# Retention values of heads 0 and 1 by seven block products ahead of the core, kept split in DRAM, with the core's heads overlapping by two chunks

## The chip, the cores and the metric

The kernel runs on one core of a Trainium2 chip. The metric is the device time of one execution in microseconds (us). TensorE is written PE, VectorE DVE, ScalarE ACT, GpSimd POOL and SyncE SP.

## The reference

A trunk of two layers works on 1024 tokens of width 1024, in fp32. Each layer has a mixer (layer 0 a gated delta net, layer 1 a retention) and a gated FFN with a short convolution, each followed by a residual and a layer norm; inputs of mixer and FFN are scaled and shifted by vectors computed from a condition `c`. The change lies in the retention of layer 1, 4 heads with 256 features in q and k and 512 in v, cut into 8 chunks of 128 tokens:

```
q, k, v, gate = jnp.split(h @ w_in, [H * dk, 2 * H * dk, 2 * H * dk + H * dv], axis=-1)
...
scores = jnp.einsum('bhncd,bhnmd->bhncm', q, k) * dmask[None, :, None]
intra = jnp.einsum('bhncm,bhnmv->bhncv', scores, v)
...
    o = jnp.einsum('bhck,bhkv->bhcv', q_n, state) * xi[None, :, :, None]
    state = (state * gamma_c[None, :, None, None]
             + jnp.einsum('bhck,bhcv->bhkv', k_n * zeta[None, :, :, None], v_n))
...
o = _standardize(o, 1e-6).reshape(b_, s, H * dv)
o = o * jax.nn.silu(gate.astype(F32))
return o.astype(h.dtype) @ w_out
```

The state passes from chunk to chunk, so the chunks of one head follow each other; heads are independent.

## The kernel before, in words

**Split operands.** An fp32 product is made of three fast matmuls: each operand is split into a high part (ACT copies it into the rounded type, L89) and a low part (DVE subtracts, L90), and low x high, high x low and high x high are summed in PSUM (`split` L88, `mm3` L108, `mma` L312).

**Seven products.** The projections for the gate and for q and k run as a 2 x 2 block product with seven instead of eight products (`strassen`, L1334). It leaves the blocks `B` of the normalized input in SBUF: 11 and 21 are the first half of the tokens (`hTb` buffers, also called `h0`), 22 the second half's upper features, T1 to T4 sums and differences (`hTa`, `aux`, `qkv`). q and k go through the rotation to DRAM (`qd`), the gate through silu to DRAM (`gd`). Then `hT[1]`, the second half of the tokens, is completed by transposing four loaded tiles `xlo`.

**The core's program.** The retention core is written as generators, which a small planner (`run`, L758) interleaves: it keeps a clock of the matmuls issued so far (`pm` and `pq` add their assumed cost), each generator yields a delay or an event that it waits for, and of those that are due the one with the lowest number goes next. The order that results on PE is fixed by dependencies (`pq`, L736). `core(h)` makes the recurrence of head h, `ret_back` the normalization and output of one chunk, and `ret_fill` is the filler that takes PE whenever no core step is due: the values of a head (`ret_v`), and behind them the first two of seven products of the out-projection (`proj_gen`). A fixed number of `qkv` buffers, counted by `take` and `give`, limits how far values run ahead: 20 buffers, two per chunk of values.

**Values.** `ret_v(h, half)` multiplies half of the tokens with the head's weights: 8 contraction tiles x 4 token tiles x 3 = 96 matmuls of 512 columns, into four `acc` banks. Four splits then give the values `vv` of four chunks, high and low. Heads 0 to 3 and two halves make 768 matmuls.

**One chunk of the core.** Two halves of the state update (3 matmuls each, `sc<-vv,kz`, each into a bank of the tag `sc`, of which there are two), read by DVE into `Sr`; the scores and transposed keys of the next chunk (`mm<-qk`, `mm<-cst,qk`) with `kz`, `sT`, `sThl`; the transposes of the chunk before (`mm<-cst,on`); the output (`sc<-vv,sThl` x3 and `sc<-Sr,qk` x2, the latter in full fp32) into an `sc` bank. `ret_back`: bn_stats and its aggregate on DVE, the power -1/2 on POOL (L2026), `on` on DVE (L2030), which frees the bank; four transposes, product with the gate (`ot`, L2051), stores to DRAM (`od`); for chunks 4 to 7 POOL forms four sums of blocks (L2062) for the out-projection, the fourth after the first store has landed.

Before, `core(h)` waits for the first values of its head and for the end of `core(h - 1)`.

Of the kernel before, what the change touches and what calls it, by code (L numbers as in the profile page):

```python
# [9 lines left out]
F32 = mybir.dt.float32  # L10
F32R = mybir.dt.float32r
# [4 lines left out]
P = 128  # L16
D = 1024
# [16 lines left out]
def trunk_kernel(ctx: ExitStack, tc, A):  # L34
# [11 lines left out]
    def tl(tag, shape, dt=F32, name=None):  # L46
        return sb.tile(shape, dt, tag=tag, name=name or tag, bufs=BUFS[tag])
# [34 lines left out]
    def hs(half):  # L82
        return slice(half * HALF, (half + 1) * HALF)
# [4 lines left out]
    def split(dst_h, dst_l, src, eng=dve):  # L88
        anchor["sp"] = act.activation(dst_h, src, AF.Copy)  # L89
        eng.tensor_tensor(dst_l, src, dst_h, ALU.subtract)  # L90
# [211 lines left out]
    def build_hT(tag, xts, scale, shift, fr=range(KT)):  # L302
        return [build_one(tag, xts, scale, shift, f) for f in fr]
# [503 lines left out]
    def give(tag, n):  # L807
        free[tag] += n
# [1106 lines left out]
    gates_ = [gate_item(u) for u in range(4, 16, 2)]  # L1915
    mixed = [(ropes if q == "r" else gates_).pop(0) for q in "rrgrgrrgrgrrgg"]
    B = strassen(h0, xts, sc_r, sh_r, [gate_item(0), gate_item(2)] + mixed, ("hTa", "aux", "qkv", "qkv", "hTa"), True)
    hT = [h0, []]
    xlo = []
    for t in range(4):  # L1920
# [2 lines left out]
        with after(("out", 0)):  # L1923
            sp.dma_start(x, xs[1][r0:r0 + P, 0:HALF])
        xlo.append(x)
    hT[1] = build_hT("hTa", xlo, sc_r, sh_r, range(4)) + B["22"]

    def ret_v(h, half):
        accs = acc4()
        for kp in range(4):  # L1930
            wh, wl = load_w(A["ret_wv"][h, kp])
            if (h, half, kp) == (RH - 1, 1, 3):
                yield after_ev(("qk", h))
                start_out()
# [38 lines left out]
        return r  # L1973

    def core(h):
        yield after_ev(("rv", h, 0), ("core", h - 1))
        if h == 1:
            bg_ada(1, 2, "row")
        q, k = load_qk(h, 0), load_qk(h, 1)
        emit(("qk", h))  # L1980
        St = None
        yield RL["q"]
        r = ret_front(h, 0, q, k)
        yield RL["f"]
        for n in range(NCH):
            if n == 4:
                yield after_ev(("rv", h, 1))
            vh, vl = va[h][n]
            Sn = None
            if n < NCH - 1:  # L1990
                kz = r["kz"]
                Sn = tl("lane", [P, 2, HALF], name="Sr")
                for j in range(2):
                    js = slice(j * P, (j + 1) * P)
                    p2 = sc_tile()
                    pm(p2, kz[:, 1, js], vh, start=True, stop=False)
                    pm(p2, kz[:, 0, js], vl, start=False, stop=False)
                    pm(p2, kz[:, 0, js], vh, start=False, stop=True)
                    if n == 0:
                        dve.tensor_copy(Sn[:, j], p2)  # L2000
                    else:
                        dve.scalar_tensor_tensor(Sn[:, j], St[:, j], gamma_c[h], p2, ALU.mult, ALU.add)
# [11 lines left out]
            give("qkv", 2)  # L2014
            yield [(-0.1, ret_back(h, n, po))]
            yield RL["c"]
            St, r = Sn, rn
        emit(("core", h))

    def ret_back(h, n, po):  # L2020
        st = tl("st", [P, 2, 6], name="rst")
        dve.bn_stats(st[:, 0], po)
        mv = tl("s8", [P, 4], name="mv")
        dve.bn_aggr(mv[:, 0:2], st[:, 0])
        dve.tensor_scalar(mv[:, 2:3], mv[:, 1:2], 1e-6, None, ALU.add)
        pool.tensor_tensor(mv[:, 3:4], mv[:, 2:3], mhalf[:, 0:1], ALU.pow)  # L2026
        if n < 4 or h == RH - 1 and n == 4:
            gains.pop(0)()
        on = tl("t2", [P, HALF], name="on")
        anchor["on"] = dve.tensor_scalar(on, po, mv[:, 0:1], mv[:, 3:4], ALU.subtract, ALU.mult)  # L2030
# [20 lines left out]
        dve.tensor_mul(ot, pt, g)  # L2051
# [7 lines left out]
        act.dma_start(blk("22"), ov[:, 1])  # L2059
        for d, x, y, op, nm in ((ov[:, 0], ov[:, 0], ov[:, 1], ALU.add, "S1"), (pv[:, 0], ov[:, 0], pv[:, 0], ALU.subtract, "S2"),  # L2060
                                (pv[:, 1], pv[:, 1], pv[:, 0], ALU.subtract, "S4"), (ov[:, 1], ov[:, 1], pv[:, 0], ALU.subtract, "S3")):
            pool.tensor_tensor(d, x, y, op)  # L2062
            (pool if n == NCH - 1 and h == RH - 1 else sp).dma_start(blk(nm), d)

    def load_qk(h, j):
# [8 lines left out]
    RL = {"v": 2.57, "q": 5.9, "f": 3.35, "p": 0.55, "c": 2.75, "b": 3.21, "o": 4.42}  # L2074
# [149 lines left out]
```

## Time and profile before

| | us |
|---|---|
| median of three runs | 2866.8 |
| lowest, highest | 2865.53, 2873.29 |
| the profiled execution | 2872.47 |
| its span | 2870.7 |
| mean granted clock of TensorE | 0.994 |
| PE busy | 2785.2 (97%) |
| DVE, ACT, POOL busy | 2183.3, 1294.0, 500.2 |

Busy time is the time in which an engine executes. PE's matmuls are pipelined: each lasts about 0.39 us and the next starts earlier, so what a matmul costs is seen between two starts. A group's row has the source line, the engine, the operation, outputs and inputs by tile name, the count, and behind the bar the busy time in us and the mean ns of one, then the idle time before them with who ended it. A row of the timeline begins with its start in us and its duration; a bracket gives the idle time before it and who ended it. A window's row has its length, busy time and count by engine, the granted clock, the share of the DMA engines and GB/s. `PEld` is the weight load, `SPq` and `ACTq` are DMA issues.

### The profile page before, as it was taken

To read this page: it belongs to the slowest core of one execution; us is meant where nothing else is said; L and a number is where in the kernel's file an instruction comes from. 1 tells how busy PE (TensorE), PEld (TensorE's weight loads), DVE (VectorE), ACT (ScalarE), POOL (GpSimd) and SP (SyncE) were. 2 spreads that over 40 slices of the span, in tenths; PEclk is the share of its full clock that TensorE was granted. 3 is DMA by queue.
4 is the path that set the end of the run, shared out by engine and by line. 5 is a ranking of instruction groups with operands and counts; after the bars stand their busy time and mean duration, and the time that the engine had idled before them with its cause. 6 is when DMAs were issued, how large, how long until landed. Compare 5 with 4: busy or idle time off the path is not lost.

```text
span 2870.7 us, 38939 instructions
## 1 busy us (share of the span) xinstructions
PE 2785.2 (97%) x13594; PEld 2277.0 (79%) x13594; DVE 2183.3 (76%) x3874; ACT 1294.0 (45%) x2377; POOL 500.2 (17%) x517
## 2 busy tenths in 40 slices
PE   8999999999999999999999999999999999999997
PEld 6787878877787788887888887777787778888886
DVE  6887678676788888778677656666788887777869
ACT  3763465344644444546433342222344644444443
POOL 0411321000023233100000002333301033332001
PEclk9999999999999999999999999999999999999999
DMA  8323242174254555945343364665854253444853
GB/s 279 101 90 115 92 140 92 61 250 150 99 180 168 192 183 172 336 126 180 128 147 119 121 204 153 200 196 160 275 194 147 74 194 132 143 139 161 320 150 118
DMA packets 254292, 465.31 MB, mean 162 GB/s; under 512 B 24400, under 2 KB 81104, under 8 KB 254096
## 3 DMA queue, kind: packets, MB, share of 16 engines
q1 hardware_dynamic: 219776, 407.50, 43.0%
q10 hardware_dynamic: 31488, 46.15, 4.4%
q0 software_dynamic: 2832, 9.18, 0.8%
q8 instruction: 107, 1.75, 0.2%
q14 instruction: 89, 0.73, 0.1%
HBM read 346.86 MB, written 115.87 MB: 161 GB/s over the span
## 4 chain that ended last, share of the span: by engine, by line
PE 56%; DVE 21%; DMA 11%; ACT 6%; issue 5%; POOL 1%; SPq 0%; ACTq 0%; DVEq 0%; POOLq 0%
PE acc L747 10%; PE acc L1340 5%; PE acc L110 4%; PE sc L747 4%; PE acc L111 4%; PE acc L112 4%; PE sc L1340 3%; PE acc L1636 3%; DMA mvw<-in_ada_w 3%; DVE o L1787 3%; DMA wr<-in_ffn_up 2%; PE mm L747 2%; DVE wb L90 2%; DVE qkv L507 2%; DVE mm L1394 1%
## 5 line engine op out<-in xcount | busy, mean ns | idle before, releaser
L747 PE MATMUL acc<-hT,wh 128*128 128x512 f32 x960 | 299.7, 393 | 0.0
L1636 PE MATMUL acc<-bb,ab 128*128 128x512 f32 x984 | 229.8, 392 | 6.5 <-DVE ab L90 4.1
L89 ACT ACTIVATE ab<-ar 128x512 fp32r<-128x512 f32 x210 | 131.1, 629 | 217.0 <-PE mm L316 55.1
L1636 PEld LDWEIGHTS acc<-bb,ab 128*128 128x128 f32 x984 | 183.0, 188 | 48.6 <-DVE ab L90 4.7
L747 PEld LDWEIGHTS acc<-hT,wh 128*128 128x128 f32 x960 | 182.5, 190 | 35.6
L1340 PE MATMUL acc<-T,wb 128*128 128x512 f32 x840 | 202.0, 389 | 0.4 <-DVE wb L90 0.4
L90 DVE TENSOR_TENSOR ab<-ar,ab 128x512 fp32r<-128x512 f32 x210 | 148.7, 715 | 68.5 <-ACT ab L89 68.1
L747 PE MATMUL acc<-hT,wl 128*128 128x512 f32 x480 | 197.3, 411 | 1.2 <-ACT sq L531 0.7
L89 ACT ACTIVATE wb<-mm 128x512 fp32r<-128x512 f32 x216 | 124.4, 597 | 163.0 <-DVE mm L1394 150.1
L1340 PEld LDWEIGHTS acc<-T,wb 128*128 128x128 f32 x840 | 157.5, 188 | 33.8 <-ACT o L1788 1.1
L90 DVE TENSOR_TENSOR wl<-wr,wh 128x1024 fp32r<-128x1024 f32 x95 | 118.6, 1249 | 74.3 <-ACT wh L89 72.6
L1818 POOL TENSOR_TENSOR o<-o 128x512 f32<-128x512 f32 x80 | 119.0, 1496 | 270.1 <-DVE o L1810 167.9
L90 DVE TENSOR_TENSOR wb<-wr,wb 128x512 fp32r<-128x512 f32 x162 | 114.2, 706 | 65.7 <-ACT wb L89 65.6
L89 ACT ACTIVATE wh<-wr 128x1024 fp32r<-128x1024 f32 x95 | 100.6, 1060 | 138.3 <-PE acc L747 61.4
L1787 DVE SCALAR_TENSOR_TENSOR o<-g,vc,o 128x512 f32<-128x512 f32 (+2 forms) x176 | 152.2, 875 | 8.9 <-ACT o L1782 7.7
L90 DVE TENSOR_TENSOR wb<-mm,wb 128x512 fp32r<-128x512 f32 x216 | 144.5, 682 | 7.4 <-ACT wb L89 7.4
L89 ACT ACTIVATE wb<-wr 128x512 fp32r<-128x512 f32 x162 | 101.2, 626 | 95.5 <-PE acc L1340 28.8
L1394 DVE TENSOR_TENSOR mm<-wr 128x512 f32<-128x512 f32 x108 | 83.9, 777 | 71.4 <-DMA wr<-in_ffn_up 58.2
L747 PE MATMUL acc<-wh,hT 128*128 128x512 f32 x384 | 134.3, 412 | 2.1 <-DVE vv L90 2.1
L1410 ACT ACTIVATE pc<-acc 128x512 f32<-128x512 f32 x143 | 84.4, 591 | 111.8 <-PE acc L1340 63.6
L252 DVE SCALAR_TENSOR_TENSOR ada<-mvw,e,ada 128x512 f32<-128x512 f32 x140 | 105.8, 755 | 24.0 <-DMA mvw<-in_ada_w 23.8
L110 PE MATMUL acc<-T,wb 128*128 128x512 f32 x292 | 114.9, 394 | 3.6 <-DVE wb L90 3.3
(677 smaller groups left out, 7356.2 us busy)
## 6 DMA issues: line engine op xcount, KB each, us to landing
wr<-in_ffn_up SPq DMA_DIRECT2D x92, 512.0 KB, 3.9
mvw<-in_ada_w SPq DMA_DIRECT2D x80, 512.0 KB, 4.3
ad<-o SPq DMA_DIRECT2D x154, 256.0 KB, 2.3
ar<-ad SPq DMA_DIRECT2D x154, 256.0 KB, 4.2
Br<-in_ffn_down SPq DMA_DIRECT2D x88, 256.0 KB, 5.2
wr<-in_ret_wv SPq DMA_DIRECT2D x32, 512.0 KB, 3.6
ar<-od SPq DMA_DIRECT2D x56, 256.0 KB, 4.5
wr<-in_gdn_wqkv SPq DMA_DIRECT2D x24, 512.0 KB, 3.9
```

Source lines behind the costliest of these rows:

```text
L89: anchor["sp"] = act.activation(dst_h, src, AF.Copy)
L90: eng.tensor_tensor(dst_l, src, dst_h, ALU.subtract)
L110: mm(acc, wl[:, k], hl[0], start=first, stop=False)
L111: mm(acc, wh[:, k], hl[1], start=False, stop=False)
L112: mm(acc, wh[:, k], hl[0], start=False, stop=last)
L252: dve.scalar_tensor_tensor(a, wr[:, kk], e[:, k:k + 1], a, ALU.mult, ALU.add)
L747: pq(pe.matmul(out, lhsT, rhs, start=start, stop=stop), cost or COST[out.shape[-1]])
L1340: return pe.matmul(*a, skip_group_check=True, **kw)
L1394: dve.tensor_tensor(t, x, y, op)
L1636: return pe.matmul(*args, skip_group_check=True, **kw)
L1787: dve.scalar_tensor_tensor(tv, gv[:, c0 - j:c1 - j], w[:, 2 - j:3 - j], tv, ALU.mult, ALU.add)
L1818: (dve if fp == 0 else pool).tensor_tensor(o[d], o[x], o[y], op)
```

## The change

Values of heads 0 and 1 are no longer filler. A new `values_01` makes them between the gate, q and k products and the core: blocks of the tokens (two halves), of the contraction (two halves) and of the columns (head 0, head 1) form a 2 x 2 block product of seven products, each of 4 operand tiles x 4 token tiles x 3 matmuls = 48. Sums of weight blocks are made on DVE (`keep`, `first`), partial results are copied out of PSUM by ACT (`part`) and added by DVE. Each chunk's values are split and both parts stored to a DRAM tile `vd` from ACT's queue (32 stores of 256 KB). `hT[1]` is completed within the sixth product.

In the core a generator `fetch_v` loads the values of heads 0 and 1 back on SP's queue (32 loads of 256 KB), at most two chunks ahead. `ret_fill` holds only heads 2 and 3. `core(h)` announces its end two chunks earlier (after the state of chunk 6 is due), and q and k of the next head are loaded at chunk 5, so the last two chunks of a head can stand among the first of the next. The out-projection's start waits for another event (`ob` of head 1).

```
+    def values_01():
...
+        def operand(p, j):
+            if p == 0:
+                src = first[j]
+            elif p == 1:
+                src = load(0, 1, j)
+            elif p == 2:
+                src = keep[j] = load(1, 0, j)
+                dve.tensor_tensor(src, src, load(1, 1, j), ALU.add)
...
+            t = tl(("wh", "wl")[(4 * p + j) % 2], [P, 2, HALF], F32R, name="wb")
+            split(t[:, 0], t[:, 1], src)
+            return t[:, 0], t[:, 1]
...
+        def put(h, n, c):
+            vv = two("qkv", F32R, "vv")
+            split(vv[0], vv[1], c)
+            for i in range(2):
+                act.dma_start(vd[h, n, i], vv[i].bitcast(F32))
...
+        for p, nm in enumerate(("11", "21", "T1", "T2", "22", "T3", "T4")):
...
+            if p == 5:
+                hT[1] = build_hT("hTa", xlo, sc_r, sh_r, range(4)) + B["22"]
...
+            for t in range(4):
+                for j in (2, 3):
+                    mma(accs[t], t, B[nm][j], ws[j], False, j == 3, pe.matmul if fresh else mm_on)
+                if p in part:
+                    act.activation(part[p][t], accs[t], AF.Copy)
+                if p in (1, 4, 5, 6):
+                    c = part[{1: 0, 4: 3, 5: 2, 6: 5}[p]][t]
+                    dve.tensor_tensor(c, accs[t], c, ALU.add)
+                    put(p // 5, t + (4 if p in (4, 5) else 0), c)
...
-    hT[1] = build_hT("hTa", xlo, sc_r, sh_r, range(4)) + B["22"]
+    values_01()
...
-                yield after_ev(("qk", h))
+                yield after_ev(("ob", 1))
...
     def core(h):
-        yield after_ev(("rv", h, 0), ("core", h - 1))
+        yield after_ev(("rv", h, 0) if h > 1 else ("vf", h, 0), ("core", h - 1))
...
+            if n == 5 and h < RH - 1:
+                qk[h + 1] = load_qk(h + 1, 0), load_qk(h + 1, 1)
+                emit(("qk", h + 1), RL["q"])
+            if n == NCH - 2:
+                emit(("core", h))
...
+            if h < 2:
+                yield after_ev(("vf", h, n))
...
-        emit(("core", h))
...
+    def fetch_v():
+        for m in range(2 * NCH):
+            yield lambda: m < used[0] + 2
+            yield from take("qkv", 2)
+            vv = two("qkv", F32R, "vv")
+            for i in range(2):
+                sp.dma_start(vv[i].bitcast(F32), vd[m // NCH, m % NCH, i])
...
-        for h in range(RH):
+        for h in range(2, RH):
...
-    run([(0.0, ret_fill())] + [(-1.0, core(h)) for h in range(RH)])
+    run([(0.0, ret_fill()), (-2.0, fetch_v())] + [(-1.0, core(h)) for h in range(RH)])
```

**Where the instructions now stand: PE in the core.** Before, each chunk of heads 0 to 2 reads as follows; `acc<-wh,hT` and `acc<-wl,hT` are value matmuls of `ret_v`, three ahead of the output and fifteen behind it (of these the first rows are shown):

```order
L747 MATMUL sc<-vv,kz 128x512 x6
L747 MATMUL mm<-qk 128x128 x2
L750 MATMUL mm<-cst,qk 128x128 x2
L750 MATMUL mm<-cst,on 128x128 x4
L747 MATMUL acc<-wh,hT 128x512
L747 MATMUL acc<-wl,hT 128x512
L747 MATMUL acc<-wh,hT 128x512
L747 MATMUL sc<-vv,sThl 128x512 x3
L747 MATMUL sc<-Sr,qk 128x512 x2
L747 MATMUL acc<-wh,hT 128x512
L747 MATMUL acc<-wl,hT 128x512
L747 MATMUL acc<-wh,hT 128x512 x2
```

In the changed kernel the chunks of head 0 and of head 1 up to chunk 4 read the same. From the output of chunk 5 of head 1 on, the rows are these (chunk 6 of head 1, then chunk 0 of head 2 with the output of chunk 7 of head 1 among its rows):

```order
L747 MATMUL sc<-vv,sThl 128x512 x3
L747 MATMUL sc<-Sr,qk 128x512 x2
L747 MATMUL sc<-vv,kz 128x512 x6
L747 MATMUL mm<-qk 128x128 x4
L750 MATMUL mm<-cst,qk 128x128 x2
L747 MATMUL sc<-vv,sThl 128x512 x3
L747 MATMUL sc<-Sr,qk 128x512 x2
L750 MATMUL mm<-cst,on 128x128 x4
L747 MATMUL sc<-vv,kz 128x512 x6
L747 MATMUL mm<-qk 128x128 x2
L750 MATMUL mm<-cst,qk 128x128 x2
L747 MATMUL sc<-vv,sThl 128x512 x3
```

No value matmul stands in them, nor in the following 9 rows of the state and output of head 2's first two chunks. Sixty value matmuls of head 2 stand ahead of the first chunk of head 0; the last quarter of the filler (second half of head 3) begins behind those rows.

**DVE at the same place.** From `on` of chunk 5 of head 1 (first row) to `on` of chunk 6; `COPY Sr<-sc` are the two halves of head 2's first state, `vv<-acc` values of head 3:

```order
L2125 TENSOR_SCALAR on<-sc,mv 128x512
L2055 TENSOR_TENSOR sT<-mm,dm 128x128
L2053 SCALAR_TENSOR_TENSOR kz<-mm,vc,kz 128x256
L2055 TENSOR_TENSOR sT<-mm,dm 128x128
L90 TENSOR_TENSOR vv<-acc,vv 128x512
L90 TENSOR_TENSOR sThl<-sT,sThl 128x128 x2
L2117 BN_STATS rst<-sc 128x6
L2146 TENSOR_TENSOR ot<-mm,gt 128x512
L2119 BN_AGGR mv<-rst 128x2
L2095 COPY Sr<-sc 128x512
L2120 TENSOR_SCALAR mv<-mv 128x1
L2125 TENSOR_SCALAR on<-sc,mv 128x512
```

Steps of two heads share one line: the copy that frees a bank for head 2 stands behind the normalization of head 1.

**ACT between the sixth and the seventh product.** `vc<-acc` are the sixth product's copies, `vd<-vv` stores, the lines L297 and `hT` the completed input, and `wb<-vr` the third and the fourth operand of the seventh product; two more of the sixth product's copies stand just ahead of these rows:

```order
L89 ACTIVATE vv<-vc 128x512
L297 ACTIVATE t_15613<-mm,fh_11999,fs_11998 128x512
L1970 DMA vd<-vv 128x512
L89 ACTIVATE vv<-vc 128x512
L297 ACTIVATE t_15623<-mm,fh_11999,fs_11998 128x512
L89 ACTIVATE hT<-t_15613 128x512
L1970 DMA vd<-vv 128x512 x2
L89 ACTIVATE hT<-t_15623 128x512
L89 ACTIVATE wb<-vr 128x512
L1970 DMA vd<-vv 128x512
L1998 ACTIVATE vc<-acc 128x512 x2
L89 ACTIVATE wb<-vr 128x512
```

Before there was no such stretch: ACT split the weights of `ret_v`, 1024 columns at a time, and the values' halves.

More of the change, by code (lines that the diff above doesn't have):

```diff
@@ L1917, in trunk_kernel, with mm_on, load, four @@
     B = strassen(h0, xts, sc_r, sh_r, [gate_item(0), gate_item(2)] + mixed, ("hTa", "aux", "qkv", "qkv", "hTa"), True)
+    vd = dr.tile([2, NCH, 2, P, HALF], F32, tag="vd", name="vd")
+    def values_01():
+        W = A["ret_wv"]
+        def mm_on(*args, **kw):
+            return pe.matmul(*args, skip_group_check=True, **kw)
+        first = []
+        for kp in range(2):
+            t = tl("wr", [P, D], name="va")
+            sp.dma_start(t, W[0, kp])
+            first += [t[:, hs(0)], t[:, hs(1)]]
+        def load(h, side, j):
+            t = tl("auh", [P, HALF], name="vr")
+            sp.dma_start(t, W[h, 2 * side + j // 2][:, hs(j % 2)])
+            return t
+        keep, made = [None] * 4, []
+        def operand(p, j):
[6 more added lines that the diff above has]
+                dve.tensor_tensor(src, src, load(1, 1, j), ALU.add)
+            elif p == 3:
+                src = keep[j]
+                dve.tensor_tensor(src, src, first[j], ALU.subtract)
+            elif p == 4:
+                src = load(0, 1, j)
+                dve.tensor_tensor(src, src, keep[j], ALU.subtract)
+            elif p == 5:
+                src = load(1, 0, j)
+                dve.tensor_tensor(src, first[j], src, ALU.subtract)
+            else:
+                src = load(1, 1, j)
+            t = tl(("wh", "wl")[(4 * p + j) % 2], [P, 2, HALF], F32R, name="wb")
+            split(t[:, 0], t[:, 1], src)
+            return t[:, 0], t[:, 1]
+        def four(tag):
+            t = [tl(tag, [P, 2, HALF], name="vc") for _ in range(2)]
+            return [t[i // 2][:, i % 2] for i in range(4)]
+        def put(h, n, c):
[3 more added lines that the diff above has]
+                act.dma_start(vd[h, n, i], vv[i].bitcast(F32))
+        steps = [(p, j) for p in range(7) for j in range(4)]
+        X = Z = None
+        part = {}
+        for p, nm in enumerate(("11", "21", "T1", "T2", "22", "T3", "T4")):
+            fresh = p in (0, 1, 2, 6)
+            if p == 0:
+                X = acc4()
+            elif fresh:
+                Z = [sc_tile(), sc_tile(), mm_tile(), mm_tile()]
+            if p == 5:
+                hT[1] = build_hT("hTa", xlo, sc_r, sh_r, range(4)) + B["22"]
+            accs = X if p in (0, 3, 5) else Z
+            ws = []
+            for j in range(4):
+                while len(made) < min(4 * p + j + 4, len(steps)):
+                    made.append(operand(*steps[len(made)]))
+                ws.append(made[4 * p + j])
+                if j < 2:
+                    for t in range(4):
+                        mma(accs[t], t, B[nm][j], ws[j], fresh and j == 0, False, pe.matmul if fresh else mm_on)
+            if p in (0, 2, 3, 5):
+                part[p] = four("lane" if p == 2 else "xT")
+            for t in range(4):
+                for j in (2, 3):
[6 more added lines that the diff above has]
+                    put(p // 5, t + (4 if p in (4, 5) else 0), c)
@@ L1975, in core @@
     def core(h):
-        yield after_ev(("rv", h, 0), ("core", h - 1))
+        yield after_ev(("rv", h, 0) if h > 1 else ("vf", h, 0), ("core", h - 1))
         if h == 1:
             bg_ada(1, 2, "row")
-        q, k = load_qk(h, 0), load_qk(h, 1)
-        emit(("qk", h))
+        if not h:
+            qk[0] = load_qk(0, 0), load_qk(0, 1)
+            emit(("qk", 0), RL["q"])
+        q, k = qk[h]
         St = None
-        yield RL["q"]
+        yield after_ev(("qk", h))
         r = ret_front(h, 0, q, k)
@@ L1985, in core @@
         for n in range(NCH):
-            if n == 4:
+            if n == 5 and h < RH - 1:
[3 more added lines that the diff above has]
+                emit(("core", h))
+            if n == 4 and h > 1:
                 yield after_ev(("rv", h, 1))
+            if h < 2:
+                yield after_ev(("vf", h, n))
             vh, vl = va[h][n]
```

6 lines of the change are left out of this document (5 added, 1 removed).

## The prediction

> **What bounds the kernel now.** I read the page first, then the busy time by stretch (windows), then the timeline of single stretches, then the groups of instructions.
>
> ```profile
> span 2870.7 us, 38939 instructions
> PE 2785.2 (97%) x13594; PEld 2277.0 (79%) x13594; DVE 2183.3 (76%) x3874; ACT 1294.0 (45%) x2377; POOL 500.2 (17%) x517
> ```
>
> TensorE (PE) is busy for 97% of the span. An edit that removes matmuls therefore pays their issue time, unless it makes PE wait somewhere. The stage that is changed runs from 1702 us (end of the gate and q/k products) to about 2045 us (last chunk of head 3):
>
> ```profile
> core 0: us, PE busy (x) PEld busy (x) DVE busy (x) ACT busy (x) POOL busy (x), PEclk, DMA share, GB/s
> 1702.00:1740.00 38.00, 37.03 (x174) 30.34 (x173) 14.67 (x19) 16.35 (x24) 0.12 (x1) 1.00 0.46 158
> 1740.00:1792.00 52.00, 52.00 (x240) 40.50 (x239) 35.98 (x67) 11.66 (x21) 17.17 (x17) 1.00 0.55 172
> 1792.00:1822.00 30.00, 29.13 (x131) 22.07 (x130) 15.34 (x27) 7.63 (x11) 12.49 (x16) 1.00 0.67 202
> 1938.00:1951.00 13.00, 11.01 (x43) 8.41 (x42) 8.71 (x18) 0.93 (x3) 1.10 (x2) 0.87 0.56 187
> 1951.00:2045.00 94.00, 93.16 (x424) 71.51 (x424) 64.19 (x120) 25.86 (x47) 32.61 (x37) 1.00 0.65 201
> ```
>
> In whole stretches PE has no idle time at all (52.00 of 52.00 us). It is idle for 0.97 + 0.87 + 1.99 + 0.84 = 4.7 us in the other four, and the 1938 row has a granted clock of 0.87. VectorE (DVE) is busy 35.98 of 52 us, ScalarE (ACT) 11.66. So the stage is bound by what PE issues; the recurrence of the core is hidden behind the value matmuls that stand between its steps.
>
> The price of a 512-column matmul is read from start to start, since the durations (0.39 us) overlap:
>
> ```profile
> 1680.81 2.88 PE L1340 MATMUL acc<-T,wb 128*128 128x512 f32 x12
> 1683.53 0.39 PE L110 MATMUL sc<-hT,wb 128*128 128x512 f32 x1
> ...
> 1774.31 1.52 PE L747 MATMUL sc<-vv,kz 128*128 128x512 f32 x6
> 1783.31 1.52 PE L747 MATMUL sc<-vv,kz 128*128 128x512 f32 x6
> ```
>
> Twelve matmuls take 1683.53 - 1680.81 = 2.72 us, so 0.2267 us each. The other two rows open two neighbouring chunks of head 0: 9.00 us apart. Between them stand 18 value matmuls (3 + 15 in the order) worth 18 x 0.2267 = 4.08 us. A chunk's own PE work is 9.00 - 4.08 = 4.92 us, and the 18 value matmuls exactly cover its waits.
>
> **1. The matmuls.** Heads 0 and 1 had 2 heads x 2 halves x 96 = 384 value matmuls. The seven products have 7 x 4 x 4 x 3 = 336. 48 go: 48 x 0.2267 = **-10.9 us**, certain as long as PE stays the bound. The 16 transposes of `xlo` move from the start to the sixth product and cost the same.
>
> **2. The products as a stage of their own.** PE needs 336 x 0.2267 = 76.2 us and about 2 us for the transposes: 78 us. What the other engines need per instruction:
>
> ```profile
> L90 DVE TENSOR_TENSOR wb<-wr,wb 128x512 fp32r<-128x512 f32 x162 | 114.2, 706 | 65.7 <-ACT wb L89 65.6
> L89 ACT ACTIVATE wb<-wr 128x512 fp32r<-128x512 f32 x162 | 101.2, 626 | 95.5 <-PE acc L1340 28.8
> L1394 DVE TENSOR_TENSOR mm<-wr 128x512 f32<-128x512 f32 x108 | 83.9, 777 | 71.4 <-DMA wr<-in_ffn_up 58.2
> L1410 ACT ACTIVATE pc<-acc 128x512 f32<-128x512 f32 x143 | 84.4, 591 | 111.8 <-PE acc L1340 63.6
> L90 DVE TENSOR_TENSOR vv<-acc,vv 128x512 fp32r<-128x512 f32 x32 | 22.0, 688 | 4.9 <-ACT vv L89 4.8
> L89 ACT ACTIVATE vv<-acc 128x512 fp32r<-128x512 f32 x32 | 19.1, 596 | 39.3 <-PE acc L747 38.3
> ...
> 1787.25 0.46 ACTq L2059 DMA_DIRECT2D od<-ot  x1
> ```
>
> ACT: 28 operand halves x 0.626, 16 copies x 0.591, 16 value halves x 0.596, 32 stores issued at 0.46, and some 5 us for `hT` = 56 us. DVE: 28 x 0.706 operand halves, 12 operand sums and 16 sums out of PSUM at 0.777, 16 x 0.688 value halves, 3 us for `hT` = 55 us. Both fit in 78. What remains is order. ACT stands in line, and each operand of the next product waits there behind copies, stores and, since only four `qkv` slots are free, the landing of earlier stores. The tightest place is the step from the sixth to the seventh product: two copies, two value halves, three stores and five activations of `hT` (about 0.6 each) stand ahead of the third operand, a store and two more copies ahead of the fourth. All but two of the first group come after the sixth product's second sum, 2.7 us before its end: -2.7 + 5.8 = 3.1 us into the seventh, with 0.626 and DVE's 0.706 the third operand is there at 4.5 (wanted at 5.4, after 24 matmuls); the fourth has 1.6 and 0.626 more on ACT and two sums and its own half, 2.3, on DVE: 7.6, wanted at 6.1, so 1.5 late. Bounds: 0 (all early) and 5 us (each of the later products late by 1); I take **+1.5 us**. The four operand sums that the order puts ahead, among the last products of the stage before, cost DVE 4 x 0.777 = 3.1 us there; bounds 0 and 3, taken **+0.5 us**.
>
> **3. Stores and fetches.** 32 stores and 32 fetches of 256 KB come on top.
>
> ```profile
> wr<-in_ret_wv SPq DMA_DIRECT2D x29, 512.0 KB, 3.6
> gt<-gd SPq DMA_DIRECT2D x30, 256.0 KB, 4.1
> ```
>
> A load of that size lands in 4.1 us in this stage, at a DMA share of 0.46 to 0.67. A fetch may be issued two chunks ahead, over 9 us at the old pace. Cost **0**, covered by that; if SyncE (SP), where a fetch stands behind other waiting transfers, loses the cover, about 1 us a chunk in the 16 chunks of two heads, 16 us at worst. The new event for the out-projection (`ob` of head 1 for `qk` of head 3) lies earlier than its use and moves nothing.
>
> **4. Where the filler runs out.** This decides the sign. Only heads 2 and 3 are left as filler: 384 matmuls, and the last 96 must wait for free `qkv` slots, that is for head 2 to begin. 288 remain for heads 0 and 1. The order spends 60 before the first chunk and 18 per chunk, so (288 - 60) / 18 = 12.7 chunks. Chunks 5 and 6 of head 1 and 0 and 1 of head 2 stand with no filler (shown with the change). What one such chunk waits for is in the timeline of head 0:
>
> ```profile
> 1786.53 0.68 DVE L2051 TENSOR_TENSOR ot<-mm,gt 128x512 f32<-128x512 f32 x1
> 1787.13 0.47 DVE L1967 SCALAR_TENSOR_TENSOR kz<-mm,vc,kz 128x256 fp32r<-128x256 f32 x1
> 1787.16 1.88 PE L747 MATMUL sc<-Sr,qk 128*128 128x512 f32 x4
> 1787.53 0.28 DVE L1969 TENSOR_TENSOR sT<-mm,dm 128x128 f32<-128x128 f32 x1
> 1789.08 0.70 DVE L2022 BATCH_NORM_STATS2 rst<-sc 128x6 f32<-128x512 f32 x1
> 1789.81 0.18 DVE L2024 BATCH_NORM_AGGREGATE mv<-rst 128x2 f32<-128x6 f32 x1
> 1790.03 0.15 DVE L2025 TENSOR_SCALAR mv<-mv 128x1 f32<-128x1 f32 x1
> 1791.46 0.74 POOL L2062 TENSOR_TENSOR ot<-ot,op 128x256 f32<-128x256 f32 x1 [1.76 <-DMA od<-ot]
> 1792.16 0.55 POOL L2026 TENSOR_TENSOR mv<-mv,mhalf 128x1 f32<-128x1 f32 x1
> 1792.75 0.81 DVE L2030 TENSOR_SCALAR on<-sc,mv 128x512 f32<-128x512 f32 x1 [2.56 <-POOL mv L2026]
> 1793.47 0.68 DVE L2002 SCALAR_TENSOR_TENSOR Sr<-Sr,sc 128x512 f32<-128x512 f32 x1
> 1793.61 0.97 PE L747 MATMUL sc<-vv,kz 128*128 128x512 f32 x3 [0.46 <-DVE on L2030]
> ```
>
> From the end of the output matmuls (L747 `sc<-Sr,qk`): bn_stats 0.70, aggregate 0.18, add 0.15, the power on GpSimd (POOL) 0.55, `on` 0.81, and the PSUM bank is free; with hand-overs 2.8 us. After that comes the next state half (3 matmuls, 0.68), `Sr` 0.68, output matmuls 0.68 + 1.71. Following the new order with these durations from the first state matmul of chunk 5 of head 1:
>
> - chunk 6, second state half: its bank is free when DVE has read the first half: idle 0.9 us.
> - head 2 chunk 0, second state half: behind `on`, DVE has `sT` 0.28, `kz` 0.47, `sT` 0.28, a value half 0.69, two halves of `sThl` (taken as `sT`), bn_stats 0.70, `ot` 0.68 and an aggregate 0.18 ahead of the copy (taken as `Sr`, 0.68) that frees the bank: 4.5 us. PE has the rest of its output matmuls (1.1), four transposes and the first half (1.1) in that time: idle 2.3.
> - head 2 chunk 1, first state half: both `sc` banks hold outputs, of head 1 chunk 7 and of head 2 chunk 0. DVE runs two bn_stats 1.40, aggregates 0.36, `ot` 0.68, a value half 0.69, adds 0.30, then the power and `on` 0.55 + 0.81: about 5.2 us with hand-overs, against 1.1 us of PE work (3 matmuls, 4 transposes): idle 4.1.
> - smaller ones (0.2, 0.35, 0.65): 1.2 us.
>
> Sum **+8.5 us**. Bounds: 4 (only the last of these, if the others overlap) and 14 (the second and third each 2.5 longer). The same crossing from head 2 to 3 has 3 + 12 fillers (3.4 us) in it, so the last gap shrinks to about 1 us and the second to about 1: **+2 us** (0 to 4). From head 0 to 1 it is fully filled.
>
> **5. The clock after a gap.**
>
> ```profile
> 1940.56 1.65 PE L747 MATMUL sc<-vv,kz 128*128 128x512 f32 x3 [1.99 <-DVE on L2030]
> ...
> 1941.00:1942.00 1.00, 1.00 (x3) 0.72 (x3) 1.00 (x2) 0.00 (x0) 0.00 (x0) 0.50 0.00 0
> 1942.00:1943.00 1.00, 1.00 (x6) 1.00 (x5) 1.00 (x3) 0.00 (x0) 0.00 (x0) 0.50 0.28 57
> ```
>
> After the wait of 1.99 us the granted clock is 0.50 for about 3 us (three matmuls took 1.65 us instead of 0.84); that lost about 1.7 us. After the 0.46 us wait at 1793.61 it stayed at 1.00 (the 1792 row above). In part 4 two gaps reach 2 us: 0 to 3.4 us. I count the 4.1 us gap alone, **+1.7 us**. [...]
>
> **6. What leaves.** The 4.7 us of idle time above and the 1.7 us at half clock belong to the old order. The wait at 1702 to 1740 goes with the old start; the boundary of heads at 1792 goes with the overlap. The 1938 gap stands behind DVE's steps for the gain row (`ada`), of which the new order runs half in head 0 and half later, so such a gap returns. Bounds 0 and -6; taken **-3 us**.
>
> Sum: -10.9 + 1.5 + 0.5 + 0 + 8.5 + 2 + 1.7 - 3 = **+0.3 us**. The profiled execution took 2872.5 us, the span of 2870.7 and 1.8 around it; the median of the three runs shown is 2866.8, 5.7 lower. By the median the new time is 2867.1, say **2867 us**: no change that a measurement can tell. It can tell about 0.3%, 8.6 us: faster is below 2858, slower above 2875.5.
>
> **Rivals.**
>
> *The starved stretch costs little.* Two heads are in flight there, and if their chains cover each other, part 4 shrinks from 10.5 to 3 us, no gap reaches 2 us (part 5 goes), and part 6 gives 5: -10.9 + 2 + 3 - 5 = -11, 2856 us. For it: the order does interleave both heads' steps. Against it: both share two `sc` banks, and DVE's line is in order. It decides if no PE gap in the stretch passes 1.5 us. Chance 0.27, the near side of forecast and rival together.
>
> *Slower: the store in the loop.* In the chain rows above GpSimd waits 1.76 us for a store (`od<-ot`) before its fourth step L2062, and the power for the next chunk stands behind it. `on` to transposes, `ot`, store landing (4.2 us from 1787.25 to 1791.46), 0.74, 0.55, 0.81 makes a loop of 9.0 to 9.4 us a chunk: hidden at 9.00 us, bare at 4.92. Five chunks at 4.3 us make 21 instead of 8.5: +13, 2880 us. The new order of GpSimd has that step ahead of the power in one of the three starved chunks, behind it in the others. It decides if PE's gaps in the stretch end on GpSimd. Chance 0.11.
>
> *Slower: half clock throughout.* If the short waits keep the clock at 0.50 over the starved stretch, its 21 us of PE work (4.92 a chunk and the transposes left over) take 42 in place of 21 + 8.5 + 1.7: +11, 2878 us. Only the one spell of 3 us speaks for it; after 0.46 us of waiting nothing happened. Chance 0.06. [...]
>
> *The change is not done as said:* the seven products wait on ACT or on stores all along (5 us or more), or fetches come late in every chunk (16 us): 2872 to 2883 us, mostly the first. Chance 0.06, half of it slower.
>
> **Numbers.** Forecast 0.50, all within 0.3%; with half of the last rival and the near side of the first, no change has 0.55. Faster 0.25, slower 0.20. The range that leaves out 2 in 10 goes from the first rival, 2856, to the second, 2880.
>
> **What would show it.** In the new profile: 48 matmuls fewer; PE without idle in the products but for 1 to 3 us near the seventh; heads 0 and 1 at 9.0 us a chunk up to chunk 4 of head 1; then a stretch of about 28 us with 8 us of gaps, the longest where head 2 enters its second chunk, released by `on` (L2125), with a granted clock of 0.50 behind it. If PE is busy throughout, the first rival holds; if GpSimd or a DMA from `vd` releases the gaps, the second or last. A difference in any stage before 1660 us would be outside this working.

## The result and the profile after

| | median us | runs | ratio to before | 95% interval |
|---|---|---|---|---|
| before | 2867.15 | 4 | | |
| changed | 2890.47 | 4 | 1.0076 | 1.0064 to 1.0089 |

The change makes the kernel about 22 us slower, where 2867 was forecast. The profiled execution of the changed kernel took 2891.28 us, 18.8 more than that of before; the latter lay 5.3 over its median. The page begins:

```profile
span 2889.5 us, 39102 instructions
PE 2783.7 (96%) x13546; PEld 2272.2 (79%) x13546; DVE 2205.8 (76%) x3918; ACT 1302.7 (45%) x2405; POOL 490.0 (17%) x517
```

PE has 48 instructions fewer (13594 before), as worked out, but only 1.5 us less busy time where 10.9 were worked out, and the span is 18.8 us longer: PE waits more, and part of its work runs at half the clock. The windows of the changed kernel, in the columns of the prediction (length, busy time by engine, granted clock, DMA share, GB/s), show where:

```profile
1702.00:1796.00 94.00, 94.00 (x428) 77.97 (x427) 56.02 (x86) 45.69 (x75) 0.00 (x0) 1.00 0.66 227
1796.00:1851.00 55.00, 52.87 (x240) 40.28 (x239) 40.78 (x74) 11.13 (x20) 17.71 (x18) 1.00 0.87 297
1851.00:1918.00 67.00, 61.88 (x269) 47.24 (x268) 40.39 (x77) 12.48 (x22) 22.98 (x27) 0.95 0.78 242
1918.00:1965.00 47.00, 38.91 (x164) 27.41 (x163) 31.14 (x65) 9.00 (x18) 22.32 (x28) 0.93 0.75 224
1965.00:1996.00 31.00, 28.08 (x122) 21.42 (x121) 22.40 (x42) 4.25 (x9) 7.43 (x9) 0.94 0.43 127
1996.00:2071.00 75.00, 66.69 (x286) 48.84 (x285) 52.01 (x100) 19.79 (x40) 26.83 (x32) 0.95 0.71 227
```

The seven products (first row) run without any idle time. From the first chunk on (1796) PE is idle in every row: 2.1, 5.1, 8.1, 2.9 and 8.3 us, 26.6 in all, and in four of these rows the granted clock is 0.93 to 0.95. A like comparison takes 1702 to 2100, which holds the whole stage in both traces: PE is idle for 8.2 us before and 27.0 now, and half the clock costs 1.7 us before and 10.5 now (PE's busy time at 0.50, halved). These 27.6 us less the 10.9 for the matmuls are 16.7 of the 18.8. (The 4.7 us of the prediction leave out 0.8 between 1822 and 1938 and the start of the out-projection.) Only the 1918 row is the starved stretch of the prediction. The list of waits (engine, line, whom it waited for, us in total, times, longest), for PE, first before and then changed:

```profile
PE sc L747 <- DVE on L2030: 2.8, 3, 2.0
```

```profile
PE sc L747 <- DVE on L2125: 15.2, 8, 4.5
PE mm L750 <- DVE sT L2055: 5.4, 2, 4.9
```

The bank that `on` frees is the main wait, as foreseen, but not mainly in starved chunks. The longest of these waits is the starved gap that the prediction put at 4.1 us:

```profile
1941.62 2.93 PE L747 MATMUL sc<-vv,kz 128*128 128x512 f32 x6 [4.54 <-DVE on L2125]
```

The longest one with filler at hand is in chunk 1 of head 1; the timeline of the changed kernel (start, duration, instruction, idle time and who ended it):

```profile
1873.31 0.15 DVE L2120 TENSOR_SCALAR mv<-mv 128x1 f32<-128x1 f32 x1
1873.68 1.31 POOL L2207 TENSOR_TENSOR xg<-xg,gb 128x512 f32<-128x512 f32 x1 [4.46 <-DMA xg<-xs]
1874.34 0.84 PE L747 MATMUL sc<-vv,kz 128*128 128x512 f32 x3
1874.92 0.74 POOL L2157 TENSOR_TENSOR ot<-ot 128x256 f32<-128x256 f32 x1
1875.61 1.28 POOL L2208 TENSOR_TENSOR xg<-xg,gb 128x512 f32<-128x512 f32 x1
1876.83 0.74 POOL L2157 TENSOR_TENSOR op<-ot,op 128x256 f32<-128x256 f32 x1
1877.51 0.57 POOL L2121 TENSOR_TENSOR mv<-mv,mhalf 128x1 f32<-128x1 f32 x1
1878.11 0.81 DVE L2125 TENSOR_SCALAR on<-sc,mv 128x512 f32<-128x512 f32 x1 [4.65 <-POOL mv L2121]
1878.97 1.65 PE L747 MATMUL sc<-vv,kz 128*128 128x512 f32 x3 [3.79 <-DVE on L2125]
```

These are the power and `on` of chunk 0's output, whose bank the state of chunk 1 needs. The power's input is ready at 1873.46, but GpSimd first makes two steps `xg` that the prediction did not look at. They prepare the **gain row**, the residual of the out-projection (`gain_step`, L2204): a block of `xs` is loaded into a `lane` buffer that it shares with the state `Sr`, multiplied and shifted on GpSimd (1.3 us each) and stored, one block in each of the chunks 0 to 3 of a head. GpSimd had stood 4.46 us for the block's load, and two block sums of head 0 (L2157) stand between. The power comes 4.0 us late, PE waits 3.8, and behind that the clock is at 0.50: the three matmuls took 1.65 us instead of 0.84. In the kernel before the same steps stood in the same place, here in the first chunk of head 1:

```profile
1823.58 1.29 POOL L2100 TENSOR_TENSOR xg<-xg,gb 128x512 f32<-128x512 f32 x1 [5.07 <-DMA xg<-xs]
1824.94 1.30 POOL L2101 TENSOR_TENSOR xg<-xg,gb 128x512 f32<-128x512 f32 x1
1826.75 0.55 POOL L2026 TENSOR_TENSOR mv<-mv,mhalf 128x1 f32<-128x1 f32 x1 [0.51 <-DVE mv L2025]
```

The wait for the load was even longer (5.07 us), but GpSimd was done 0.51 us before the power's input came: some 65 value matmuls between two heads had let head 0's block sums, stores and loads run out. That slack is gone once head 1 follows closely.

### The profile page after: what moved, and what is told of

It is laid out like the page before. It is cut to its first block, busy times and chain, and to the rows that moved or that the text cites. A ratio compares the mean times of both kernels' runs of the same rounds, so it can differ in the third digit from the quotient of the medians.

```text
span 2889.5 us, 39102 instructions
## 1 busy us (share of the span) xinstructions
PE 2783.7 (96%) x13546; PEld 2272.2 (79%) x13546; DVE 2205.8 (76%) x3918; ACT 1302.7 (45%) x2405; POOL 490.0 (17%) x517
## 4 chain that ended last, share of the span: by engine, by line
PE 60%; DVE 18%; DMA 10%; ACT 5%; issue 4%; POOL 2%; SPq 0%; ACTq 0%; DVEq 0%; POOLq 0%
PE acc L747 7%; PE acc L1340 6%; PE acc L1636 4%; PE acc L110 4%; PE acc L111 4%; PE acc L112 4%; PE sc L747 3%; PE sc L1340 3%; DVE o L1787 2%; DMA mvw<-in_ada_w 2%; PE mm L747 2%; DMA wr<-in_ffn_up 2%; DVE qkv L507 2%; DVE wb L90 2%; PE sc L110 1%
## 5 line engine op out<-in xcount | busy, mean ns | idle before, releaser
L1340 PE MATMUL acc<-T,wb 128*128 128x512 f32 x840 | 202.0, 389 | 0.4 <-DVE wb L90 0.4
L90 DVE TENSOR_TENSOR wl<-wr,wh 128x1024 fp32r<-128x1024 f32 x79 | 97.8, 1238 | 49.7 <-ACT wh L89 46.0
L89 ACT ACTIVATE wh<-wr 128x1024 fp32r<-128x1024 f32 x79 | 83.6, 1060 | 86.2 <-PE acc L341 47.7
L110 PE MATMUL acc<-T,wb 128*128 128x512 f32 x292 | 114.5, 392 | 4.5 <-DVE wb L90 4.4
L111 PE MATMUL acc<-T,wb 128*128 128x512 f32 x292 | 113.7, 389 | 0.0
```

Of the source, the lines that this page charges most:

```text
L110: mm(acc, wl[:, k], hl[0], start=first, stop=False)
L111: mm(acc, wh[:, k], hl[1], start=False, stop=False)
L1340: return pe.matmul(*a, skip_group_check=True, **kw)
```

## The experiments

The kernel before measured 2867 to 2871 us in the batches, so ratios are compared; 0.001 is 2.9 us. Theory S (starvation) is the prediction's own mechanism. Theory Q, later G (the gain steps on GpSimd), came from the timeline above.

**Heads apart.**

```
-            if n == NCH - 2:
-                emit(("core", h))
...
             St, r = Sn, rn
+        emit(("core", h))
```

> The products for heads 0 and 1 stay, a head starts when the last chunk of the head before has been issued. Theory Q (queues: while two heads are in flight, the products of the output blocks and the gain row on GpSimd, the transfers on SyncE and the splits on ScalarE of one head stand ahead of the other head's steps): the long waits where heads meet (6.7 us at 1875, about 10 us from 2002 to 2030 in the changed kernel) go, the stretch without filler stays at about 13 us: 2873 us, 2868 to 2879. Theory S (starvation: the loss is where no value matmuls are left): four chunks without filler at about 3.4 us each are no cheaper than what is there now: 2890 us, 2886 to 2896.

Measured: 1.0086 (1.0071 to 1.0101). Theory Q as I put it fails. q and k are still loaded ahead, so the heads follow each other closely even without overlap, and the waits stay; chunk 1 of head 1 again:

```profile
1876.59 1.26 POOL L2206 TENSOR_TENSOR xg<-xg,gb 128x512 f32<-128x512 f32 x1 [3.73 <-DMA xg<-xs]
1877.93 1.26 POOL L2207 TENSOR_TENSOR xg<-xg,gb 128x512 f32<-128x512 f32 x1
1879.15 0.55 POOL L2120 TENSOR_TENSOR mv<-mv,mhalf 128x1 f32<-128x1 f32 x1
1879.73 0.81 DVE L2124 TENSOR_SCALAR on<-sc,mv 128x512 f32<-128x512 f32 x1 [4.81 <-POOL mv L2120]
```

The same gain step is in the way with the heads one after the other. Two heads at once are not the cause of this wait.

**Overlap alone.** `values_01` and `fetch_v` are out, `ret_fill` makes all four heads again:

```
-    values_01()
+    hT[1] = build_hT("hTa", xlo, sc_r, sh_r, range(4)) + B["22"]
...
-        for h in range(2, RH):
+        for h in range(RH):
```

> The values of heads 0 and 1 are filler again as in the kernel before (no products, no trip through DRAM), the heads overlap by two chunks. All chunks have filler. Theory Q: each of the three places where heads meet loses 5 to 8 us: 2882 us, 2876 to 2890. Theory S: no chunk starves, so as the kernel before: 2867 us, 2862 to 2870.

Measured: 1.0047 (1.0030 to 1.0064), 13 us slower than before although no chunk lacks filler: theory S alone fails. The longest wait of PE is the same chain:

```profile
1822.73 1.28 POOL L2205 TENSOR_TENSOR xg<-xg,gb 128x512 f32<-128x512 f32 x1 [4.31 <-DMA xg<-xs]
1824.08 1.26 POOL L2206 TENSOR_TENSOR xg<-xg,gb 128x512 f32<-128x512 f32 x1
1825.30 0.55 POOL L2119 TENSOR_TENSOR mv<-mv,mhalf 128x1 f32<-128x1 f32 x1
1826.75 0.98 PE L747 MATMUL sc<-vv,kz 128*128 128x512 f32 x3 [3.14 <-DVE on L2123]
```

**Gain steps later in a head.**

```
-        if n < 4 or h == RH - 1 and n == 4:
+        if n in (2, 3, 4, 5) or h == RH - 1 and n == 6:
             gains.pop(0)()
```

> The changed kernel with the gain-row steps of GpSimd (1.3 us each, two per chunk) in chunks 2 to 5 of a head in place of 0 to 3, so out of the two chunks in which heads overlap. Theory Q: the waits of 3.96 us at 1875 and 1.48 us at 1900 with the half clock behind them (8.3 us together) go, and some 2 us of the wait at 1937: 2881 us, 2877 to 2885. Theory S: no change, 2890 us, 2887 to 2893.

Measured: 1.0057 (1.0042 to 1.0072), 5 us better than the change where theory Q named 9; the interval overlaps that of the change, so this run alone does not show a gain. Its trace does: chunk 1 of head 1 takes 9.00 us in place of 15.96; gaps of PE of 2.2 us before 1849.7 (head 0), which the change did not have, and of 1.9 and 2.5 us before 1912.5 and 1926.9 take a part back.

**q and k early.** Head 0's q and k are loaded during the seventh product, so that the core can begin some 13 us earlier:

```
+                if p == 6 and j == 2:
+                    qk[0] = load_qk(0, 0), load_qk(0, 1)
...
-            qk[0] = load_qk(0, 0), load_qk(0, 1)
-            emit(("qk", 0), RL["q"])
+            emit(("qk", 0))
...
-            emit(("vf", m // NCH, m % NCH), RL["l"])
+            emit(("vf", m // NCH, m % NCH), RL["l"] if m > 1 else 0.0)
```

> The changed kernel with the q and k of head 0 and the first two chunks of values fetched during the seventh product, so that some 45 value matmuls are not spent before the first chunk and nearly every chunk up to head 2 has its 18. Theory S: of the about 13 us lost between 1918 and 1955 some 10 go: 2880 us, 2876 to 2884. Theory Q: only the part of those waits that is not due to GpSimd's line goes, 3 to 5 us, and the places where heads meet keep theirs: 2886 us, 2884 to 2890.

Measured: 1.0063 (1.0048 to 1.0078), 4 us better than the change and near what theory Q expected, but within the noise: the interval overlaps that of the change. A flaw of the edit hid a part: SP asked for the first values only behind the filler's weights, and PE stood 6.05 us before the first chunk, with half the clock for 7 us behind it.

**Half of each fetch.**

```
-            for i in range(2):
-                sp.dma_start(vv[i].bitcast(F32), vd[m // NCH, m % NCH, i])
-            va[m // NCH].append(vv)
+            sp.dma_start(vv[0].bitcast(F32), vd[m // NCH, m % NCH, 0])
+            va[m // NCH].append((vv[0], vv[0]))
```

> The changed kernel, but of each value chunk of heads 0 and 1 only the high half comes back from DRAM (256 KB in place of 512) and stands in for the low half as well: the low halves are left out of the result, TensorE's instructions stay the same. Theory T (transfers: the fetches make the others late, the gain row's loads landed in 4.5 us over heads 0 and 1 where they took 2.7): 4 to 8 us faster than the changed kernel, ratio to the kernel before 1.0050 to 1.0062, and the wait at 1875 shrinks to under 2 us. Theory O (only the order and the number of steps on the engines count): no change, 1.0070 to 1.0083.

Measured: 1.0080 (1.0065 to 1.0095). Theory T is out. The median landing of the gain row's load (last column, us) before, changed, and with half the fetch:

```profile
xg<-xs SPq DMA_DIRECT2D x15, 256.0 KB, 2.7
```

```profile
xg<-xs SPq DMA_DIRECT2D x16, 256.0 KB, 4.0
```

```profile
xg<-xs SPq DMA_DIRECT2D x16, 256.0 KB, 3.8
```

It does land later in the new order, but hardly because of the fetched bytes, and the time does not follow them. One sign that theory T named nearly came, since the wait in chunk 1 of head 1 shrank from 3.79 to 2.18 us; but waits of 2.22 and 2.07 us stood in head 0 in its place, where the change had none over 1.21.

**No GpSimd steps in the gain row.**

```
             x, c, rs, gb = gx.pop()
-            pool.tensor_tensor(x, x, gb[0], ALU.mult)
-            pool.tensor_tensor(x, x, gb[1], ALU.add)
             sp.dma_start(xg[0][rs, hs(c)], x)
```

> The changed kernel without the two GpSimd steps of each gain-row block (the row is stored as it was loaded: the scale and shift of the gain row are left out). Its loads and stores stay. Theory G (the power on GpSimd stands behind a gain step that waits for its load): the waits at 1875 and 1900 with the half clock behind them go (8 us), and 2 to 3 us near 1937: ratio 1.0040 to 1.0050. Rival: other steps are nearly as late (stores, loads, DVE's line), so under 3 us: 1.0066 to 1.0080.

Measured: 1.0040 (1.0027 to 1.0052): 0.0036, some 10 us, go, as theory G said (5 to 15 us with the two intervals). Chunk 1 of head 1 in this run:

```profile
1870.53 0.15 DVE L2120 TENSOR_SCALAR mv<-mv 128x1 f32<-128x1 f32 x1
1871.03 0.55 POOL L2121 TENSOR_TENSOR mv<-mv,mhalf 128x1 f32<-128x1 f32 x1
1871.61 0.81 DVE L2125 TENSOR_SCALAR on<-sc,mv 128x512 f32<-128x512 f32 x1 [0.93 <-POOL mv L2121]
1872.48 0.96 PE L747 MATMUL sc<-vv,kz 128*128 128x512 f32 x3 [0.25 <-DVE on L2125]
```

The power now starts 0.35 us after its input is there, and PE waits 0.25 us in place of 3.79. From 1862 to 1902, where heads 0 and 1 meet, the changed kernel lost 5.1 us to idle time and 3.1 to half the clock; this run has 0.6 us of idle time there and no half clock (a granted clock of 1.00 from 1871 to 1899).

**q, k and the first values early.** As the run with q and k early, and in the same place:

```
+                    for m in range(2):
+                        vv = two("qkv", F32R, "vv")
+                        for i in range(2):
+                            sp.dma_start(vv[i].bitcast(F32), vd[0, m, i])
+                        va[0].append(vv)
```

> As the run with early q and k, but the first two value chunks are asked for by SyncE right behind q and k, ahead of the weights of the filler: the wait of 6.2 us before the first chunk, with the half clock of 5 us behind it, goes. Theory S (starvation costs some 10 us): ratio 1.0038 to 1.0050. Rival (what starves the chunks is worth less than 5 us, other waits step in): 1.0058 to 1.0070.

Measured: 1.0049 (1.0033 to 1.0066): 0.0027, some 8 us, go (2 to 14 us with the two intervals). This is what theory S expected. The windows from chunk 5 of head 1 to chunk 2 of head 2, of the changed kernel and of this run:

```profile
1918.00:1954.60 36.60, 28.67 (x121) 20.11 (x119) 24.13 (x52) 6.72 (x14) 19.08 (x25) 0.91 0.71 210
```

```profile
1914.00:1952.00 38.00, 34.17 (x155) 24.71 (x154) 25.32 (x52) 7.63 (x15) 19.20 (x25) 1.00 0.75 226
```

PE's idle time falls from 7.9 to 3.8 us, and the half clock, under which PE worked for about 5 us, is gone, which is worth 2.5 us more. In the same trace, though, head 0 has 5.0 us of gaps and 3.0 us of half-clock loss between 1782 and 1822, and the whole stage loses only 2 us less than in the changed kernel. The profiled execution (2889.57 us) was the slowest of the four. So the gain in the starved stretch is seen, but not how it makes the 8 us of the ratio.

**Both together** (this edit and the late gain steps).

> Both edits together: q, k and two value chunks early, gain-row steps in chunks 2 to 5. If the two causes are separate, their gains add: ratio 1.0015 to 1.0040. If both only shift the same wait, no better than the better of the two alone: 1.0045 or more.

Measured: 1.0032 (1.0020 to 1.0043). The two gains alone were 0.0027 and 0.0019, which would leave 1.0030: they add, and 1.0045 or more is ruled out.

**Control: the old order without the GpSimd steps** (the same edit of `gain_step` in the kernel before).

> Control: the kernel before without the two GpSimd steps of each gain-row block (scale and shift of the gain row left out). Theory G (the gain steps hurt only where heads follow each other closely): in the old order every one of them ends before the power's input is there, so no change: ratio 0.9985 to 1.0005. Rival (the gain steps cost the same in any order): 0.9960 to 0.9970, and the gain found for the changed kernel would be no part of what the change did.

Measured: 0.9999 (0.9987 to 1.0010). The steps cost nothing in the old order; their cost belongs to the change.

**Overlap alone without the GpSimd steps.**

> Values of heads 0 and 1 as filler as before, heads overlapped by two chunks, gain row without its GpSimd steps (scale and shift left out). Theory G: of the 1.0047 that the overlap alone cost, 0.0025 to 0.004 goes: 1.0005 to 1.0025. Rival (the overlap costs by filler operands that come late from SyncE, or by the shared banks): 1.0035 to 1.0050.

Measured: 1.0018 (1.0009 to 1.0027). Of the 0.0047 that the overlap alone cost, 0.0029 were the gain steps.

**q, k and values early, no GpSimd steps.**

> The changed kernel with q, k and two value chunks early and without the GpSimd steps of the gain row (scale and shift left out). If starvation (0.0027) and gain steps (0.0036) are separate causes: 1.0076 - 0.0063 = 1.0013, 1.0000 to 1.0025. If one hides behind the other: 1.0030 or more.

Measured: 1.0011 (1.0001 to 1.0021); the sum of separate causes was 1.0013. The early loads and the gain steps are two causes that add. The first of PE's waits that are left:

```profile
PE sc L747 <- DVE on L2143: 4.3, 5, 2.6
```

`on` holds PE for 4.3 us in place of 15.2.

**A complete kernel with buffers of its own for the gain row.** The sixteen blocks are written ahead of `values_01`, in `hTb` buffers that are free there, together with the early q, k and values:

```
+    for c in range(2):
+        for r in range(NCH):
...
+            x = tl("hTb", [P, HALF], name="xg")
...
+            pool.tensor_tensor(x, x, gb[0], ALU.mult)
+            pool.tensor_tensor(x, x, gb[1], ALU.add)
+            sp.dma_start(xg[0][r * P:r * P + P, hs(c)], x)
```

> q, k and two value chunks early, and the gain-row blocks complete, but no longer one per chunk in buffers shared with the state: all sixteen are written ahead of the products with buffers of their own, so that their loads need not wait for a state buffer of the core; nothing is left out. If a gain step hurts because GpSimd stands still until its load has landed (theory G, the wait): near the run without the GpSimd steps, ratio 1.0005 to 1.0022. If the 2.6 us of its two steps ahead of the power are enough (theory G, the work): 1.0028 to 1.0045, as with early q and k and late gain steps.

Measured: 1.0028 (1.0017 to 1.0040), on the border between the two expectations. The order did not take the steps where they were written: they ran from 1892 to 1960, and where heads 1 and 2 meet three of them (a multiplication and two shifts), and a block sum behind them that is not shown, stand in a row ahead of a power whose input had been ready for 3.9 us:

```profile
1913.66 1.26 POOL L1927 TENSOR_TENSOR xg<-xg,gb 128x512 f32<-128x512 f32 x1 [1.18 <-DMA xg<-xs]
1914.88 2.53 POOL L1928 TENSOR_TENSOR xg<-xg,gb 128x512 f32<-128x512 f32 x2
1918.05 0.55 POOL L2151 TENSOR_TENSOR mv<-mv,mhalf 128x1 f32<-128x1 f32 x1
```

Chunk 1 of head 1 is free of it (9.48 us), the place where heads 1 and 2 meet is not. Whether the wait for the load or the 2.6 us of work hurts more is left open.

## Why the prediction was wrong

By its own parts:

1. *Matmuls*, -10.9: right. 48 fewer, and PE has no idle time in the products.
2. *Products as a stage*, +2: nothing to be seen (94.00 busy of 94.00). The bound of zero was the right one.
3. *Stores and fetches*, 0: right in the time. Half the fetched bytes change nothing (1.0080 against 1.0076).
4. *Where the filler runs out*, +8.5: right in place and size. The stretch has 7.9 us of idle time, with 4.54 in the gap put at 4.1. Loading early, which takes most of the starvation away, gave 0.0027, some 8 us.
   *Crossing from head 2 to 3*, +2 (0 to 4): too small. The window of the crossing has 6.1 us without PE and 1.7 us of half-clock loss, and its longest wait is of a kind that I did not look for:

```profile
1996.00:2031.00 35.00, 28.93 (x126) 20.62 (x125) 25.42 (x51) 8.17 (x17) 16.27 (x20) 0.95 0.75 234
```

```profile
2013.50 0.46 SPq L1473 DMA_DIRECT2D ar<-od  x1
...
2018.64 0.63 ACT L89 ACTIVATE ab<-ar 128x512 fp32r<-128x512 f32 x1 [6.71 <-DMA ar<-od]
...
2019.70 0.46 ACT L2052 ACTIVATE kz<-mm,vc 128x256 fp32r<-128x256 f32 x1
...
2020.91 0.28 DVE L2055 TENSOR_TENSOR sT<-mm,dm 128x128 f32<-128x128 f32 x1
...
2021.33 0.77 PE L750 MATMUL mm<-cst,on 128*128 128x128 f32 x4 [4.86 <-DVE sT L2055]
```

   The filler has moved on to the out-projection; ACT stands 6.71 us for its load `ar`, and `kz` of the core stands behind it, then `sT`, then PE. No run took this one away.

   *"From head 0 to 1 it is fully filled"*, 0: **this is the step that failed.** PE had its value matmuls there, and still lost 8.2 us (5.1 idle, 3.1 by the clock). Filler covers a chain only as long as the chain is no longer than the chunk. Of the chain I priced the GpSimd power at 0.55 us and took the 2.8 us between output and free bank as fixed, without asking what stands ahead of the power on GpSimd. Without the gain steps the changed kernel loses 0.0036 less, some 10 us, the largest part of the 23 us by which the forecast missed that any run isolates; in the old order the same steps cost nothing.
5. *Half clock*, +1.7 (0 to 3.4): too small, since there were more gaps that brought it on. That of two gaps only the longer one would cost was my estimate. Spells at 0.50 lie at 1878.3 to 1885.2, 1939.8 to 1946.6, 1977.3 to 1980.7, 2021.7 to 2025.1 and 2059.2 to 2062.7. PE works in 21 us of them, so 10.5 us are lost, 8.8 more than before.
6. *What leaves*, -3: did not come. The gap behind the condition's row (`ada`, which the prediction calls the gain row; it is not `xg`) is back, longer than before (2.92 us before 1977.73, row below): on DVE, `on` stands behind a step of `ada` that waits 2.11 us for its load. And the other half of its DVE steps, which ran at 1440 before, stands in head 0 now and costs 1.2 us before 1814. Its buffers (`xT`) hold the products' kept parts until then; that reading is from the trace alone.

Of the rivals, the store in the loop was nearest: GpSimd's line makes the power late. But I let it decide only in the five starved chunks and by the store of `ot`, while it decided where heads meet and by the gain row. Its signal, PE's gaps ending on GpSimd, was looked for one step too near: PE waits for `on` on DVE, and only `on`'s own wait names GpSimd.

In sum, in ratios: -0.0038 for the matmuls, +0.0027 starvation, +0.0036 gain steps make 0.0025 of the measured 0.0076. The other 0.005, about 15 us, is waits that no run took apart. In the trace of the changed kernel, idle time and clock together, they are 7.8 us at the crossing to head 3, 4.4 at the `ada` steps, 3.9 where the out-projection starts (2044 to 2071) and 2.1 in head 0, together 18.2, against 9.9 in the whole stage before. That is some 8 of the 15 us; 5.3 more are the distance of the profiled execution of before from its median, and the rest stays open. The causes of these waits are read from the trace, not shown by a run. With both known causes away, and the gain row's arithmetic with them, 1.0011 is left, so no kernel here beats the one before.

## What to carry to other kernels

When filler is taken out between two stages, list for each engine what the old gap let run dry there, loads and side work too, and look at the slack of each in-order line ahead of the critical step; the slack of 0.51 us here was gone with the next change. A wait that ends on DVE is followed back one instruction further before it is priced. An edit that removes a side task from both the old and the new order tells at once whether the task's cost belongs to the change.

## What the runs showed of the hardware

Gaps shorter than expected took the clock down. In the changed kernel waits of 2.92 and 3.79 us did, but so did two of 0.81 and 1.43 us with 0.96 us of work between them:

```profile
1977.73 1.65 PE L747 MATMUL sc<-vv,kz 128*128 128x512 f32 x3 [2.92 <-DVE on L2125]
2056.60 0.96 PE L747 MATMUL acc<-bb,ab 128*128 128x512 f32 x3 [0.81 <-DVE ab L90]
2058.99 1.46 PE L747 MATMUL acc<-bb,ab 128*128 128x512 f32 x3 [1.43 <-DVE ab L90]
2060.25 2.65 PE L747 MATMUL sc<-vv,kz 128*128 128x512 f32 x6
```

The last six matmuls, 1.52 us at full clock, took 2.65. The length of a gap does not decide: a single wait of 1.21 us, before 1814.07, was followed by three matmuls in 0.96 us, as at full clock, and so was the wait of 3.14 us with the overlap alone (0.98 us, row 1826.75 above), while 1.99 us was enough in the kernel before.

What stands ahead of every spell looked at is little work of PE. The five spells of the changed kernel begin at 1878.33, 1939.77, 1977.31, 2021.69 and 2059.23, that is 18, 11, 13 and 11 times 3.413 us apart, and last 6.83, 6.83, 3.41, 3.41 and 3.41 us. In the 3.41 us ahead of each, PE was busy for 0.26, 0.72, 0.91, 0.36 and 1.21 us, and for 1.47 us ahead of the one in the kernel before (1937.10 to 1940.51, the spell from there to 1943.92). In the 3.41 us up to 1814.07, where the wait of 1.21 us had no spell behind it, it was busy for 2.20. So here a single wait cost 1.7 us at half clock (1.99 us) or nothing (1.21 and 3.14 us); at which length of a gap, or at which share of work, the clock falls is not shown.

The rival of a half clock throughout did not come: from 1918 to 1954.6 the granted clock was 0.91.
